# Ten low parts of a split-precision encoder layer move from VectorE to GpSimd, two units are loaded later, and three evictions are made in two steps

## The chip, the cores and the metric

The kernel runs on one core of one Trainium2 chip. The core has TensorE (PE in the profile, with its weight loads as PEld), VectorE (DVE), ScalarE (ACT), GpSimd (POOL) and SyncE (SP, which issues most DMAs here). The metric is the device time of one execution in microseconds. Before the change it is 1222.64 us, the median of three runs (1221.2 to 1223.08).

## The reference

One encoder layer over 1024 tokens of width 1024, in fp32: an adaLN-modulated norm, a gated spatial MLP and a windowed attention, merged by two gates; then the output projection `w_o`, a second norm and a SwiGLU feed-forward of width 2816. The change lies at the projection and the start of the feed-forward:

```python
mod = jax.nn.silu(c) @ w_ada + b_ada
sh1, sc1, gt1, sh2, sc2, gt2 = jnp.split(mod[:, None, :], N_MOD, axis=-1)
...
merged = jax.nn.sigmoid(gate_a) * a_out + jax.nn.sigmoid(gate_b) * b_out
x = x + gt1 * (merged @ w_o)

h2 = rmsnorm(x, norm2_g) * (1.0 + sc2) + sh2
f_gate, f_up = jnp.split(h2 @ w_ffn_in, 2, axis=-1)
x = x + gt2 * ((jax.nn.silu(f_gate) * f_up) @ w_ffn_out)
```

## The kernel before

**Split operands.** TensorE multiplies in the reduced format fp32r. Each fp32 operand is split into a high part, which ACT casts, and a low part, the operand less its high part, which DVE subtracts. `multiply` forms high times high, low times high and high times low, three matmuls of 128 by 512 for each of four slices of the contraction: one product is twelve matmuls.

**Seven products.** The large matrix multiplications are done by a seven-product scheme on 2 by 2 blocks, so sums and negated sums of blocks are formed first (also on DVE). The products are named by their token block: B11, B21, T1, T2, T3, T4 and B22. In the `w_o` stage the first two are called M1 and M2. A pair p stands for two row blocks of 128 output channels. Several products add into the same PSUM bank, and DVE reads the bank out after each of them (an eviction) into the rows of x: TensorE may start the next product on a bank only once it has been read.

**Units.** 1024 columns of weights make a unit. `fetch` loads it into one of three raw buffers, `make` adds the cast (`wh`) and the low part (`wl`), each in one of three buffers. The `w_o` stage uses the units 0, A, B and C with a number; A and C come from `sO`, sums of blocks of `w_o` that were stored earlier. It also prepares the first units of the feed-forward: g0 and g1 (the gate weights of groups 0 and 1), the raw tile of g2, and f0 and f1 (groups 4 and 5), which have a buffer of their own, called `first`, in the space of the tile T2.

**The planner.** `out_products` doesn't write down an order. It adds each operation to a `Plan` with its engine (V, A, T, D for loads on SP, G for POOL), a cost, and what it reads and writes. `Plan.order` first takes TensorE's products end to end as due times, walks back from them to a latest time for every operation, and then places operations greedily by the earliest start, ties by the latest time. The engines T and D keep the order in which they were added; V, A and G may take any ready operation. The table `COST` holds durations, `WAIT` what passes between an operation's end and its use, for loads one value, 3.4 us. The result is a fixed order per engine.

**The stage in order.** M1 and M2 for the four pairs; T2, T3 and T4 for pairs 0 and 1, then for 2 and 3; T1 and B22 in the same way. Squares of the finished rows are summed (ACT squares, DVE adds to `ss`); after the first T1 TensorE sums the columns of `ss` (`at<-ones,ss`), DVE scales the result (`ms`), POOL takes the power (`rcol`) and TensorE spreads it over the partitions (`at<-ident,rcol`, called the spread below). DVE multiplies the rows of the first half by it (`mid<-mid,mod,at`) and ACT and DVE form the high and low parts of the normed block (`h`). POOL issues the stores of the finished rows to `x1d`. Behind the plan come the first feed-forward products (f, i): (0,0), (0,1), a second pair of column sums and spread for the other half, (1,0), (1,1) to (5,1), and then (0,3), (1,3), (0,2), (1,2) and so on. `prep(f, u, part)` prepares their further units, part 0 the sums and the cast, part 1 the low part.

Most operations are recorded by one helper, so the profile puts them all at line 145, DMA issues at lines 199, 204, 1257 and 1260. The functions to look for are `Plan`, and inside `out_products` `fetch`, `make`, `accumulate` and the two loops over products, and `prep`.

Of the kernel before, what the change touches and what calls it, by code (L numbers as in the profile page):

```python
# [8 lines left out]
F32 = mybir.dt.float32  # L9
# [7 lines left out]
P = 128  # L17
# [23 lines left out]
class Plan:  # L41


    COST = {"v512": 0.6, "v1024": 1.14, "p512": 0.66, "a512": 0.52, "a1024": 0.95, "small": 0.2,
            "load": 0.4, "mm": 2.72, "few": 0.45, "pow": 1.5}
    WAIT = {"V": 0.08, "A": 0.08, "T": 0.4, "D": 3.4, "G": 0.1}

    def __init__(self):
        self.ops, self.last, self.users = [], {}, {}
# [1 line left out]
    def add(self, eng, cost, fn, reads=(), writes=()):  # L51
        n = len(self.ops)
        deps = set()
        for r in reads:
            if r in self.last:
                deps.add(self.last[r])
        for w in writes:
            deps.update(self.users.get(w, ()))
            if w in self.last:
                deps.add(self.last[w])  # L60
        for r in reads:
            self.users.setdefault(r, []).append(n)
        for w in writes:
            self.last[w], self.users[w] = n, []
        self.ops.append((eng, self.COST[cost], fn, deps))

    def order(self, free):

        n = len(self.ops)
        late = [1e9] * n  # L70
        t = 0.0
        for i, (eng, cost, _, _) in enumerate(self.ops):
            if eng == "T":
                late[i] = t
                t += cost
        for i in reversed(range(n)):
            eng, cost, _, deps = self.ops[i]
            for j in deps:
                e, c = self.ops[j][:2]
                late[j] = min(late[j], late[i] - c - self.WAIT[e])  # L80
        queues = {e: [i for i in range(n) if self.ops[i][0] == e] for e in "VATDG"}
        now = {e: free.get(e, 0.0) for e in queues}
        done, start = {}, {}
        while len(start) < n:
            best = None
            for e, q in queues.items():
                for i in q[:1] if e in "TD" else q:
                    deps = self.ops[i][3]
                    if all(j in done for j in deps):
                        at = max([now[e]] + [done[j] for j in deps])  # L90
                        key = (max(at, now[e] + 0.3), late[i], i)
                        if best is None or key < best[0]:
                            best = (key, e, i, at)
            _, e, i, at = best
            queues[e].remove(i)
            start[i] = at
            now[e] = at + self.ops[i][1]
            done[i] = now[e] + self.WAIT[e]
        return sorted(range(n), key=lambda i: (start[i], i))

    def run(self, free):
# [6 lines left out]
def kernel(  # L108
# [1380 lines left out]
    def out_products(merged):  # L1489
# [53 lines left out]
        def fetch(key, parts):  # L1543
            r = f"raw{count['raw'] % 3}"
            count["raw"] += 1

            def go():
                tiles[key] = wpool.tile([P, UNIT], F32, tag="raw", name=nm("raw"))
                for cs, src in parts:
                    load(tiles[key][:, cs], src)  # L1550
            add("D", "load", go, [], [r])
            return r

        def make(key, parts, to=None):
            r = fetch(key, parts)
            w = to
            if to is None:
                w = f"w{count['w'] % 3}"
                count["w"] += 1

            def hi():
                if key not in units:
                    units[key] = wtiles()
                A.copy(units[key][0], tiles[key])
            add("A", "a1024", hi, [r], [w + "h"])
            add("V", "v1024", lambda: split_low(tiles[key], *units[key]), [r, w + "h"], [w + "l"])
            names[key] = w

        names = {}
# [32 lines left out]
            add("T", "mm", go, [w + "h", w + "l"] + [f"{t}{x}{k}" for x in "hl" for k in KS],  # L1602
                ["b" + str(p) if b == "b" else "a" + str(p)])

        def accumulate(get, tn, p, b, sc, d):
            def go():
                t = get()
                V.scalar_tensor_tensor(out=t, in0=banks[p, b], scalar=sc[:, d : d + 1], in1=t,
                                       op0=ALU.mult, op1=ALU.add)
            add("V", "p512", go, [f"{'b' if b == 'b' else 'a'}{p}"], [tn])  # L1610

        sq = {}
        seen = set()
# [1 line left out]
        def square(get, tn, hf, d):  # L1615
            if hf not in seen:
                seen.add(hf)

                def go():
                    sq[hf] = ss_tile()[:, :HALF]  # L1620
                    A.activation(sq[hf], get(), AF.Square)
                add("A", "a512", go, [tn], ["ss"])
            else:
                q = f"t{count['t'] % 4}"
                count["t"] += 1
                key = ("q", hf, d)

                def go():
                    tiles[key] = tmp()
                    A.activation(tiles[key], get(), AF.Square)  # L1630
                add("A", "a512", go, [tn], [q])
                add("V", "v512", lambda: V.tensor_tensor(sq[hf], sq[hf], tiles[key], op=ALU.add),
                    [q], ["ss"])
            add("G", "load", lambda: store(x1d[d * P : (d + 1) * P, hf * HALF : (hf + 1) * HALF], get()),
                [tn], [f"x1d{hf}{d}"])

        need("0", 2)
# [2 lines left out]
            add("D", "load", lambda p=p: load(c11[p], x_rows(0, 2 * p)), [], [f"c{p}"])  # L1640
        blocks()
        first = [(0, "M1"), (1, "M1"), (0, "M2"), (2, "M1"), (1, "M2"), (3, "M1"), (2, "M2"), (3, "M2")]
        for n, (p, name) in enumerate(first):
            product(p, name)
            if n == 2:
                need("0", 3)
            elif n in (4, 6, 7):
                need(*{4: ("A", 0), 6: ("A", 1), 7: ("B", 0)}[n])
            accumulate(lambda p=p: c11[p], f"c{p}", p, "a" if name == "M1" else "b", gt, 2 * p)
            if name == "M2":  # L1650
                square(lambda p=p: c11[p], f"c{p}", 0, 2 * p)

# [3 lines left out]
        def new_rows(hf, q, old):  # L1656
            def go():
                if hf == 0 and q == 0:
                    h2[0] = [[hid(), hid()], [hid(), hid()]]
                (x1B if hf else h2m).append(midt(F32, 4))  # L1660
            add("D", "load", go, [], [f"{old}{k}" for k in KS] + [f"{'gh'[hf]}{d}" for d in range(4 * q, 4 * q + 4)])
            for d in range(4 * q, 4 * q + 4):
                if hf or d % 2:
                    add("D", "load", lambda d=d: load(row(hf, d), x_rows(hf, d)), [], [rn(hf, d)])

        def even_rows(q):
            for d in (4 * q, 4 * q + 2):
                add("D", "load", lambda d=d: load(row(0, d), x1d[d * P : (d + 1) * P, :HALF]),
                    [f"x1d0{d}"], [rn(0, d)])

        new_rows(1, 0, "x0")
# [9 lines left out]
        for n, (p, name) in enumerate(second):  # L1681
            product(p, name)
            if n == 2:
                need("A", 2)
            elif n == 3:
                need("A", 3)
                new_rows(1, 1, "m1")
            elif n == 5:
                need("B", 2)
                new_rows(0, 1, "x1")  # L1690
            elif n == 7:
                add("D", "load", new_firsts, [], [f"T2{x}{k}" for x in "hl" for k in KS]
                    + [f"f{i}{x}" for x in "hl" for i in range(2)])
                make(("f", 0), [(all_, w_gate[EARLY - 2])], "f0")
            elif n == 8:
                even_rows(0)
                need("C", 0)
            elif n == 9:
                make(("f", 1), [(all_, w_gate[EARLY - 1])], "f1")
                need("C", 1)  # L1700
                even_rows(1)
            elif n == 11:
                need("C", 2)
            d = 2 * p + (name != "T2")
            hf = int(name != "T4")
            accumulate(lambda hf=hf, d=d: row(hf, d), rn(hf, d), p, "a", gt if name == "T2" else ngt, d)
            if name == "T4":
                square(lambda d=d: row(0, d), rn(0, d), 0, d)

# [37 lines left out]
        for n, (p, name) in enumerate(third):  # L1747
# [15 lines left out]
            elif n == 6:  # L1763
                make(("g", 1), [(all_, w_gate[1])])
                fetch(("g", 2), [(all_, w_gate[2])])
            d = 2 * p + (name == "T1")
            accumulate(lambda d=d: row(1, d), rn(1, d), p, "c", ngt if name == "T1" else gt, d)
            square(lambda d=d: row(1, d), rn(1, d), 1, d)
        for q in range(2):
            add("T", "mm", None, [f"h{x}{k}" for x in "hl" for k in range(4 * q, 4 * q + 4)]  # L1770
                + [names["g", 0] + x for x in "hl"], [])
        add("T", "few", None, ["ss"], [])
        plan.run({"V": 2.5, "A": 1.5, "T": 0.0})
        sums.extend((sq[0], sq[1]))
        early.extend(units[k, i] for k in "fg" for i in range(2))
# [36 lines left out]
    def prep(f, u, part):  # L1812
# [11 lines left out]
            A.copy(U[f, u][0], (g, ws, ws, a22[0] if f == 0 else r[:, Q:])[u])  # L1824
            return
        h, l = U[f, u]
        V.tensor_tensor(l, (g, ws, ws, a22[0] if f == 0 else r[:, Q:])[u], h.bitcast(F32), op=ALU.subtract)
        if u == 2:
            load_gate(f + 3)
        if u == 3 and f or (f, u) == (0, 2):  # L1830
# [489 lines left out]
```

## Time and profile before

| | us |
|---|---|
| median of three runs | 1222.64 |
| the profiled execution | 1221.94 |
| its span in the profile | 1220.2 |
| PE busy | 1211.0 |
| DVE busy | 928.5 |
| ACT busy | 582.4 |
| POOL busy | 150.6 |

Rows of the timeline give the start in us from the span's start, the duration in us, engine, line, operation, tile written <- tiles read, shape and count; in brackets the idle time just before it and what ended it. Rows that are grouped by line give busy us and the mean of one in ns. Tiles in PSUM are called `mm` and `at`; all others named here lie in SBUF. A row of the table by stages gives the stretch, its length, the busy us of PE, PEld, DVE, ACT and POOL with the number of instructions, the granted clock of TensorE, the busy share of the DMA engines and GB/s.

### The profile page before, as it was taken

How to read it: one execution, taken by the hardware profiler on the slowest of the kernel's cores; microseconds unless marked ns; L12 is line 12 of the kernel's file. 1: busy time of each engine (PE TensorE's matmuls, PEld its weight loads, DVE VectorE, ACT ScalarE, POOL GpSimd, SP SyncE). 2: the span in 40 equal slices, each digit the busy share in tenths (PEclk: the TensorE clock that was granted, in tenths of full speed). 3: DMA queues.
4: the chain of work that ended last, by engine and by line, in shares of the span. 5: the costliest groups of instructions: out<-in, count | busy, mean ns of one | idle time of the engine just before them, and what ended most of it. 6: DMA issues, size and time to landing. Idle time of an engine off the chain costs nothing.

```text
span 1220.2 us, 15626 instructions
## 1 busy us (share of the span) xinstructions
PE 1211.0 (99%) x5653; PEld 1007.2 (83%) x5653; DVE 928.5 (76%) x1504; ACT 582.4 (48%) x954; POOL 150.6 (12%) x182
## 2 busy tenths in 40 slices
PE   9999999999999999999999999999999999999998
PEld 7888888888888888877888888888888888888887
DVE  8999977789978776897997767675676766765646
ACT  5667865367855443644553333333333334433341
POOL 0024323024322000001100001000000000000001
PEclk9999999999999999999999999999999999999999
DMA  9752169653277233477313446455555449995552
GB/s 363 284 180 99 35 217 358 248 216 134 104 259 240 96 117 103 148 233 266 103 49 122 172 157 223 173 192 187 190 190 199 163 155 372 394 354 190 190 172 104
DMA packets 78096, 236.54 MB, mean 194 GB/s; under 512 B 8898, under 2 KB 9154, under 8 KB 72772
## 3 DMA queue, kind: packets, MB, share of 16 engines
q1 hardware_dynamic: 63028, 163.20, 38.6%
q0 software_dynamic: 14992, 72.36, 15.8%
q8 instruction: 44, 0.72, 0.3%
q14 instruction: 32, 0.26, 0.1%
HBM read 176.28 MB, written 59.24 MB: 193 GB/s over the span
## 4 chain that ended last, share of the span: by engine, by line
PE 93%; DVE 4%; issue 1%; DMA 1%; ACT 1%; POOL 0%; SPq 0%; DVEq 0%; ACTq 0%; POOLq 0%
PE mm L145 47%; PE at L145 46%; DVE mid L145 2%; DMA raw<-in_w_q_dram 1%; DVE wl L145 1%; DMA mid<-in_xA_dram 0%; DVE ss L145 0%; DVE h L145 0%; DVE ws L145 0%; ACT wh L145 0%; DVE t L145 0%; DVE tt1l L145 0%; ACT mid L145 0%; ACT h L145 0%; DVE b22l L145 0%
## 5 line engine op out<-in xcount | busy, mean ns | idle before, releaser
L145 DVE TENSOR_TENSOR wl<-raw,wh 128x1024 fp32r<-128x1024 f32 (+1 forms) x135 | 159.0, 1182 | 61.7 <-ACT wh L145 61.1
L145 ACT CAST wh<-raw 128x1024 fp32r<-128x1024 f32 (+1 forms) x149 | 152.2, 1023 | 112.1 <-PE mm L145 39.9
L145 PE MATMUL mm<-mid,wh 128*128 128x512 f32 x640 | 197.7, 390 | 0.8 <-DVE mid L145 0.8
L145 PEld LDWEIGHTS mm<-mid,wh 128*128 128x128 f32 x640 | 119.8, 188 | 25.8 <-DVE mid L145 1.2
L145 PE MATMUL mm<-wh,h 128*128 128x512 f32 x384 | 124.7, 397 | 0.5 <-ACT h L145 0.5
L145 PE MATMUL mm<-mid,wl 128*128 128x512 f32 x320 | 124.7, 390 | 0.0
L145 PE MATMUL mm<-h,wh 128*128 128x512 f32 x304 | 94.4, 392 | 0.0
L145 PE MATMUL at<-h,wh 128*128 128x512 f32 x304 | 93.9, 390 | 0.0
L145 PEld LDWEIGHTS mm<-wh,h 128*128 128x128 f32 x384 | 70.8, 188 | 14.2 <-ACT h L145 0.9
L145 DVE TENSOR_TENSOR wl<-ws,wh 128x1024 fp32r<-128x1024 f32 (+1 forms) x54 | 60.8, 1125 | 24.2 <-ACT wh L145 24.1
L145 ACT CAST wh<-ws 128x1024 fp32r<-128x1024 f32 (+1 forms) x54 | 52.5, 973 | 42.9 <-DVE ws L145 28.0
L145 PE MATMUL mm<-wl,h 128*128 128x512 f32 x192 | 71.2, 391 | 0.0
L145 PEld LDWEIGHTS mm<-mid,wl 128*128 128x128 f32 x320 | 60.1, 188 | 12.6
L145 PEld LDWEIGHTS at<-h,wh 128*128 128x128 f32 x304 | 56.9, 188 | 11.7
L145 PEld LDWEIGHTS mm<-h,wh 128*128 128x128 f32 x304 | 56.6, 188 | 11.6
L145 ACT ACTIVATE t<-t 128x512 f32<-128x512 f32 x46 | 28.4, 631 | 71.2 <-DVE t L145 71.2
L145 DVE TENSOR_TENSOR ol<-raw,oh 128x1024 fp32r<-128x1024 f32 x30 | 36.6, 1224 | 31.4 <-ACT oh L145 29.8
L145 PE MATMUL mm<-h,wl 128*128 128x512 f32 x152 | 59.4, 391 | 0.0
L145 PE MATMUL at<-h,wl 128*128 128x512 f32 x152 | 59.3, 390 | 0.0
L145 ACT ACTIVATE xs<-xs 128x512 f32<-128x512 f32 x21 | 13.3, 632 | 94.5 <-DVE xs L145 94.5
L145 ACT CAST oh<-raw 128x1024 fp32r<-128x1024 f32 x30 | 31.6, 1053 | 44.8 <-PE at L145 21.5
L145 PE MATMUL at<-wl,wh 128*128 128x512 f32 (+1 forms) x136 | 52.7, 388 | 0.0
(296 smaller groups left out, 2882.0 us busy)
## 6 DMA issues: line engine op xcount, KB each, us to landing
mid<-in_w_ada_dram SPq DMA_DIRECT2D x28, 512.0 KB, 8.3
raw<-in_w_gate_dram SPq DMA_DIRECT2D x28, 512.0 KB, 3.7
tA<-hid POOLq DMA_DIRECT2D x11, 1024.0 KB, 4.4
tB<-hid POOLq DMA_DIRECT2D x11, 1024.0 KB, 5.0
wo<-in_w_out_dram POOLq DMA_DIRECT2D x22, 512.0 KB, 5.9
wS<-wo POOLq DMA_DIRECT2D x11, 1024.0 KB, 5.2
raw<-wS SPq DMA_DIRECT2D x44, 256.0 KB, 3.4
raw<-tB SPq DMA_DIRECT2D x44, 256.0 KB, 5.2
```

The costliest lines, as they stand in the source:

```text
L145: ins = f(*args, **kw)
```

## The change

Four edits go together.

- **Ten low parts on POOL.** In `make` the units A0, A3, C2, C3, f0 and f1 get their low part by POOL's `tensor_tensor`; in `prep` the units (0,1), (0,2), (1,1) and (1,2) do.
- **Two units later.** f0 and f1 were loaded during the second group of products (T2, T3, T4); now they are loaded during the third (T1, B22).
- **Three evictions in two steps.** The first evictions of M1 of the pairs 1, 2 and 3 read their bank by an ACT copy with the scale, and DVE then adds two SBUF tiles, instead of one DVE operation that reads PSUM.
- **Landing times by kind.** The planner's table of waits has single loads, pairs of loads, loads of rows, stores and steps without work apart; the waits are kept per operation, and due times for the first feed-forward products are added.

In the built program TensorE's instructions and their order are the same. DVE has eleven rows fewer, ACT's and DVE's orders change from the M2 products on. On SP, the loads of the four units C are no longer mixed with those of f0 and f1; the two loads of `w_up` stand ahead of C3, and g0 is followed by f0, g1, g2, f1. On POOL the ten subtractions stand between the stores of `x1d` and the two powers `rcol`: A0 ahead of all stores, A3 behind the first, C2 just ahead of the first power, C3 and f0 behind the first two stores after it, f1 two stores ahead of the second power, the other four behind it.

```diff
-            "load": 0.4, "mm": 2.72, "few": 0.45, "pow": 1.5}
-    WAIT = {"V": 0.08, "A": 0.08, "T": 0.4, "D": 3.4, "G": 0.1}
+            "load": 0.4, "pair": 0.8, "row": 0.4, "none": 0.0, "store": 0.6, "g1024": 2.35, "mm": 2.72, "few": 0.45, "pow": 1.5}
+    WAIT = {"V": 0.08, "A": 0.08, "T": 0.4, "G": 0.1, "load": 3.5, "pair": 4.8, "row": 4.6, "none": 0.0, "store": 4.0}
...
+        POOL_LOWS = (('A', 0), ('A', 3), ('C', 2), ('C', 3), ('f', 0), ('f', 1),)
...
-            add("V", "v1024", lambda: split_low(tiles[key], *units[key]), [r, w + "h"], [w + "l"])
+            if key in POOL_LOWS:
+                add("G", "g1024", lambda: G.tensor_tensor(units[key][1], tiles[key], units[key][0].bitcast(F32), op=ALU.subtract), [r, w + "h"], [w + "l"])
+            else:
+                add("V", "v1024", lambda: split_low(tiles[key], *units[key]), [r, w + "h"], [w + "l"])
...
-        def accumulate(get, tn, p, b, sc, d):
+        def accumulate(get, tn, p, b, sc, d, through=False):
+            bank = f"{'b' if b == 'b' else 'a'}{p}"
+            if through:
+                q = f"t{count['t'] % 4}"
+                count["t"] += 1
+                key = ("e", tn)
+
+                def copy():
+                    tiles[key] = tmp()
+                    A.activation(tiles[key], banks[p, b], AF.Identity, scale=sc[:, d : d + 1])
+
+                def go():
+                    t = get()
+                    V.tensor_tensor(t, tiles[key], t, op=ALU.add)
+                add("A", "a512", copy, [bank], [q])
+                add("V", "v512", go, [q], [tn])
+                return
...
+        THROUGH = (('M1', 1), ('M1', 2), ('M1', 3),)
...
-                make(("f", 0), [(all_, w_gate[EARLY - 2])], "f0")
...
-                make(("f", 1), [(all_, w_gate[EARLY - 1])], "f1")
...
+            if n == 4:
+                make(("f", 0), [(all_, w_gate[EARLY - 2])], "f0")
+            if n == 6:
+                make(("f", 1), [(all_, w_gate[EARLY - 1])], "f1")
...
+        for key in ("g", 1), None, None, None, None, ("f", 0), None, ("f", 1):
+            add("T", "mm", None, [names[key] + x for x in "hl"] if key else [], [])
...
-        V.tensor_tensor(l, (g, ws, ws, a22[0] if f == 0 else r[:, Q:])[u], h.bitcast(F32), op=ALU.subtract)
+        eng = G if (f, u) in ((0, 1), (0, 2), (1, 1), (1, 2),) else V
+        eng.tensor_tensor(l, (g, ws, ws, a22[0] if f == 0 else r[:, Q:])[u], h.bitcast(F32), op=ALU.subtract)
```

More of the change, by code (lines that the diff above doesn't have):

```diff
@@ L64, in add @@
             self.last[w], self.users[w] = n, []
-        self.ops.append((eng, self.COST[cost], fn, deps))
+        self.ops.append((eng, self.COST[cost], fn, deps, self.WAIT.get(cost, self.WAIT.get(eng))))
     def order(self, free):
@@ L71, in order @@
         t = 0.0
-        for i, (eng, cost, _, _) in enumerate(self.ops):
+        for i, (eng, cost, *_) in enumerate(self.ops):
             if eng == "T":
@@ L76, in order @@
         for i in reversed(range(n)):
[L77 to L80, printed above, removed]
+            for j in self.ops[i][3]:
+                late[j] = min(late[j], late[i] - self.ops[j][1] - self.ops[j][4])
         queues = {e: [i for i in range(n) if self.ops[i][0] == e] for e in "VATDG"}
@@ L97, in order @@
             now[e] = at + self.ops[i][1]
-            done[i] = now[e] + self.WAIT[e]
+            done[i] = now[e] + self.ops[i][4]
         return sorted(range(n), key=lambda i: (start[i], i))
@@ L1550, in go @@
                     load(tiles[key][:, cs], src)
-            add("D", "load", go, [], [r])
+            add("D", "load" if len(parts) == 1 else "pair", go, [], [r])
             return r
+        POOL_LOWS = (('A', 0), ('A', 3), ('C', 2), ('C', 3), ('f', 0), ('f', 1),)
         def make(key, parts, to=None):
@@ L1609, in go @@
                                        op0=ALU.mult, op1=ALU.add)
-            add("V", "p512", go, [f"{'b' if b == 'b' else 'a'}{p}"], [tn])
+            add("V", "p512", go, [bank], [tn])
         sq = {}
@@ L1633, in square @@
                     [q], ["ss"])
-            add("G", "load", lambda: store(x1d[d * P : (d + 1) * P, hf * HALF : (hf + 1) * HALF], get()),
+            add("G", "store", lambda: store(x1d[d * P : (d + 1) * P, hf * HALF : (hf + 1) * HALF], get()),
                 [tn], [f"x1d{hf}{d}"])
@@ L1648, in out_products @@
                 need(*{4: ("A", 0), 6: ("A", 1), 7: ("B", 0)}[n])
-            accumulate(lambda p=p: c11[p], f"c{p}", p, "a" if name == "M1" else "b", gt, 2 * p)
+            accumulate(lambda p=p: c11[p], f"c{p}", p, "a" if name == "M1" else "b", gt, 2 * p, (name, p) in THROUGH)
             if name == "M2":
@@ L1660, in go @@
                 (x1B if hf else h2m).append(midt(F32, 4))
-            add("D", "load", go, [], [f"{old}{k}" for k in KS] + [f"{'gh'[hf]}{d}" for d in range(4 * q, 4 * q + 4)])
+            add("D", "none", go, [], [f"{old}{k}" for k in KS] + [f"{'gh'[hf]}{d}" for d in range(4 * q, 4 * q + 4)])
             for d in range(4 * q, 4 * q + 4):
                 if hf or d % 2:
-                    add("D", "load", lambda d=d: load(row(hf, d), x_rows(hf, d)), [], [rn(hf, d)])
+                    add("D", "row", lambda d=d: load(row(hf, d), x_rows(hf, d)), [], [rn(hf, d)])
         def even_rows(q):
             for d in (4 * q, 4 * q + 2):
-                add("D", "load", lambda d=d: load(row(0, d), x1d[d * P : (d + 1) * P, :HALF]),
+                add("D", "row", lambda d=d: load(row(0, d), x1d[d * P : (d + 1) * P, :HALF]),
                     [f"x1d0{d}"], [rn(0, d)])
@@ L1691, in out_products @@
             elif n == 7:
-                add("D", "load", new_firsts, [], [f"T2{x}{k}" for x in "hl" for k in KS]
+                add("D", "none", new_firsts, [], [f"T2{x}{k}" for x in "hl" for k in KS]
                     + [f"f{i}{x}" for x in "hl" for i in range(2)])
-                make(("f", 0), [(all_, w_gate[EARLY - 2])], "f0")
             elif n == 8:
@@ L1705, in out_products @@
             hf = int(name != "T4")
-            accumulate(lambda hf=hf, d=d: row(hf, d), rn(hf, d), p, "a", gt if name == "T2" else ngt, d)
+            accumulate(lambda hf=hf, d=d: row(hf, d), rn(hf, d), p, "a", gt if name == "T2" else ngt, d,
+                       (name, p) in THROUGH)
             if name == "T4":
```

## The prediction

> **What bounds the kernel now.** I read the page first, then the stretch of the w_o stage by engine, then TensorE's own rows wherever it waits, and last the rows of DVE and POOL where both work at once. TensorE is busy nearly all the span:
>
> ```profile
> PE 1211.0 (99%) x5653; PEld 1007.2 (83%) x5653; DVE 928.5 (76%) x1504; ACT 582.4 (48%) x954; POOL 150.6 (12%) x182
> 500.00:525.00 25.00, 25.00 (x111) 20.32 (x110) 23.67 (x35) 19.00 (x32) 0.00 (x0) 1.00 0.50 157
> 525.00:570.00 45.00, 42.74 (x194) 34.68 (x193) 38.87 (x54) 16.17 (x21) 6.51 (x11) 1.00 0.82 280
> 570.00:590.00 20.00, 20.00 (x91) 16.31 (x89) 19.78 (x30) 13.08 (x19) 3.25 (x6) 1.00 0.38 130
> 590.00:622.00 32.00, 31.69 (x148) 26.15 (x147) 29.44 (x43) 15.05 (x23) 1.04 (x1) 1.00 0.28 94
> ```
>
> The stage rows give, in turn, PE, weight loads, DVE, ACT, POOL, clock. The clock is full, TensorE never far behind, and DVE almost full: 23.67 of 25, 19.78 of 20, 29.44 of 32. TensorE's waits in the stage:
>
> ```profile
> 530.02 0.39 PE L145 MATMUL mm<-tt2h,wl 128*128 128x512 f32 x1
> 531.18 0.74 PE L145 MATMUL mm<-mid,wh 128*128 128x512 f32 x2 [0.78 <-DVE mid L145]
> 561.05 0.39 PE L145 MATMUL mm<-tt1h,wl 128*128 128x512 f32 x1
> 561.75 1.05 PE L145 MATMUL at<-ones,ss 128*128 128x1 f32 x8 [0.31 <-DVE ss L145]
> 565.28 0.39 PE L145 MATMUL mm<-tt1h,wl 128*128 128x512 f32 x1
> 566.84 1.16 PE L145 MATMUL at<-ident,rcol 128*128 128x128 f32 x8 [1.17 <-POOL rcol L145]
> 589.40 0.39 PE L145 MATMUL at<-h,wl 128*128 128x512 f32 x1
> 589.77 1.02 PE L145 MATMUL at<-ones,ss 128*128 128x1 f32 x8
> 613.47 2.88 PE L145 MATMUL mm<-h,first 128*128 128x512 f32 x12
> 616.66 3.00 PE L145 MATMUL at<-h,first 128*128 128x512 f32 x12 [0.31 <-DVE mid L145]
> ```
>
> A product is 12 matmuls, and 613.47 plus 12 steps of 0.227 is 616.19: 2.72 us a product. Against the step of 0.227, the waits are 0.93 us before T3 of pair 0 (its bank is read by the eviction of T2), 0.47 before the first column sums, 1.33 before the spread of rcol, 0.14 before the second column sums, and 0.47 at product (5,1), which waits for the bank of the spread. With half a microsecond of cold starts behind them that is all the change can win: under 4 us.
>
> **What each edit costs.** The matmuls and their order stay the same. Ten low parts leave DVE for POOL. Three evictions lose their PSUM operand on DVE and gain a copy on ACT. The units f0 and f1 are loaded, cast and split later. The rest reorders the queues.
>
> ```profile
> L145 POOL TENSOR_TENSOR wl<-raw,wh 128x1024 fp32r<-128x1024 f32 x14 | 33.7, 2407 | 0.7
> 517.84 4.90 DVE L145 SCALAR_TENSOR_TENSOR mid<-mid,mid 128x512 f32<-128x512 f32 x8
> 522.65 1.22 DVE L145 TENSOR_TENSOR wl<-raw,wh 128x1024 fp32r<-128x1024 f32 x1
> 523.79 0.74 DVE L145 SCALAR_TENSOR_TENSOR xs<-mm,mod,xs 128x512 f32<-128x512 f32 x1
> 524.45 0.74 DVE L145 SCALAR_TENSOR_TENSOR hs<-mm,mod,hs 128x512 f32<-128x512 f32 x1
> 518.55 0.62 ACT L145 CAST mid<-mid 128x512 fp32r<-128x512 f32 x1 [2.66 <-DVE mid L145]
> 519.08 1.05 ACT L145 CAST wh<-raw 128x1024 fp32r<-128x1024 f32 x1
> L145 ACT COPY t<-mm 128x512 f32<-128x512 f32 x2 | 1.2, 583 | 0.0
> raw<-in_w_gate_dram SPq DMA_DIRECT2D x28, 512.0 KB, 3.7
> ```
>
> On DVE, from start to start, an SBUF operation of 512 columns takes 0.60 (4.90 for eight), a low part 1.14 (522.65 to 523.79), an eviction 0.66. So DVE gives up 10 x 1.14 = 11.4 us, and 3 x 0.06 by the evictions. POOL takes 2.41 each, 24 us, and has little else to do here (0.00, 6.51, 3.25 and 1.04 in the four stretches). The three copies cost ACT 0.58 each; it has 6 us free in the first 25. Two of them come ahead of A0's cast at 519.08, where ACT idles 2.66 us for DVE, and the third ahead of A1's, which DVE reaches later still: nothing. Without that idle time A0's cast would be 1.2 late. The two loads of 512 KB land 3.7 us after issue; on SP's queue they move behind the last sO units and both w_up loads, and wait for POOL to free their buffer. Their products are the last four of the first feed-forward groups, over 20 us later, so the loads themselves cost nothing. The stores of x1d now queue behind POOL's low parts by up to 2.4 us, and SP's reload of those rows waits for them, with C0 behind it; the rows are first used at the norm, C0 by T1, each some 10 us later: nothing. The landing times change only the planner's order.
>
> If that were all, I would add up the waits. It is not, because of what DVE and POOL do to each other when each reads two SBUF operands:
>
> ```profile
> 104.43 2.42 POOL L145 TENSOR_TENSOR wl<-raw,wh 128x1024 fp32r<-128x1024 f32 x1
> 104.52 1.89 DVE L145 TENSOR_TENSOR pL<-at,pH 128x512 fp32r<-128x512 f32 x3
> 106.32 0.55 DVE L145 TENSOR_TENSOR es<-rows,nmx 128x4 f32<-128x4 f32 x1
> 322.44 2.42 POOL L145 TENSOR_TENSOR wl<-raw,wh 128x1024 fp32r<-128x1024 f32 x1
> 323.73 1.15 DVE L145 TENSOR_TENSOR es<-rows,nmx 128x4 f32<-128x4 f32 x1
> 122.92 0.16 DVE L145 TENSOR_TENSOR es<-rows,nmx 128x4 f32<-128x4 f32 x1
> 304.84 1.28 POOL L145 TENSOR_TENSOR mid<-xs,mid 64x512 fp32r<-64x512 f32 x1 [4.71 <-ACT mid L145]
> 330.04 1.28 DVE L145 TENSOR_TENSOR t<-t,rows 128x512 f32<-128x512 f32 x2
> 330.86 1.61 POOL L145 TENSOR_TENSOR mid<-xs,mid 64x512 fp32r<-64x512 f32 x1 [3.79 <-ACT mid L145]
> ```
>
> The tiny es sum takes 0.16 alone. Started inside a POOL low part it takes 0.55 and 1.15, and ends when POOL does: 106.87 against 106.85, 324.88 against 324.86. The three pL operations, whose first operand lies in PSUM, run beside the same POOL operation at their usual 0.60. The other way round, POOL's 1.28 becomes 1.61 behind a pair of DVE operations on SBUF. So a POOL low part stops DVE's SBUF operations until it ends, and waits for them to begin. The 14 low parts that POOL already has lie beside PSUM reads; the ten new ones lie in a stage where most DVE work (low parts, sums, negated sums) reads SBUF twice. Each then costs DVE between nothing (all beside evictions and scalings) and 2.41, and saves 1.14.
>
> What stays open is when POOL gets in while DVE runs such operations back to back. At 330.86 it came in the second of a pair and waited to the end of the run. I take that: POOL enters at DVE's next PSUM operation, which it then overlaps, so 1.75 us of block (2.41 less 0.66). The other end, entry at the next operation's end, is a rival.
>
> The sum, along TensorE. A0 is cast by 520.1; DVE streams to 522.65, so POOL runs from 522.7 to 525.1. Behind it DVE has four lows of T3 and three of T4 (0.60 each), the lows of A1 and B0 (1.14) and T2's eviction: 7 x 0.60 + 2 x 1.14 + 0.66 = 7.14, to 532.25; T3 starts at 532.4 instead of 531.18: +1.2. A3 enters beside the eviction of T3 of pair 1 and ends at 542.0; five SBUF operations, six evictions and the low of B2 (3.0 + 3.96 + 1.14) then reach 550.1, while TensorE is ready for T3 of pair 2 at 548.8: +1.4. C2 starts when T4 of pair 3 is evicted and stored, 562.6, some 0.2 before the last sum of squares is ready; the sum waits until 565.0, and the column sums start 1.95 late instead of 0.47: +1.5. The spread of rcol no longer waits, since nothing slow stands before it on DVE: -1.3. Then DVE has 23 operations of 0.66, seven of 0.60 and two low parts to the last sum of squares of the other half, 21.7 us from 569.7, with 1.8 of block by C3, 1.75 by f1, none by f0 (it falls on scalings) and 0.4 of small waits: 595.4. TensorE, from the spread at 569.5, with eight products and 0.3 before B22 of pair 2, is there at 592.5: +0.3 and +2.9, less 0.1 that it waits there today. In the feed-forward groups two of the four lows fall before the last use of the spread; with 1.14 saved and some 1.2 blocked each, (5,1) waits as today: 0. Together 1.2 + 1.4 + 1.5 - 1.3 + 0.3 + 2.8 = +5.9.
>
> The profiled execution took 1221.94 us for its span of 1220.2; the median of the three runs is 1222.64, 0.7 above, and I set the sum on the median: 1228.5 us.
>
> The Trainium skill (SBUF — State Buffer, Who interferes with whom) says that a DVE instruction with two SBUF inputs contends with a GpSimd instruction that reads SBUF, and that whichever issues first keeps the pair for its whole length. The es rows agree; on a run of DVE operations no row here decides, and by that rule POOL would enter at the next operation's end, which is the second rival.
>
> **Rivals.** First, faster: DVE loses no more than it saves, because the blocks fall on evictions, scalings and idle time. Then DVE reaches T2's eviction at 529.8 and T3 starts at 530.66 (0.5 won); the sums are in time (0.5), rcol too (1.3), (5,1) as well with its cold start (0.6), and 0.1: 3.0, so 1219.6 us. It decides where the block per low part is under 1.14 us. For it speaks f0, against it the es rows. Chance 0.18.
>
> Second, POOL enters at every operation's end. A0 then blocks 2.4 instead of 1.8 (T3 +1.9), and C3 and f0 run back to back inside the four lows of h, so T1's eviction ends at 585.4 and B22 of pair 2 waits 3.4 instead of 0.3: 5.9 + 0.7 + 3.1 + 0.5 in the chain, 1232.8 us. Chance 0.25.
>
> Third, little changes: races go the other way. If C2 starts behind the last sum (a matter of 0.2 us) and f1's split falls in a break of DVE, 1.5 and 2.4 go: +2.0, 1224.6 us. Chance 0.12.
>
> **The numbers.** My forecast has 0.45, its own range is 1225.5 to 1232. What counts as the same is 0.2%, 2.4 us. The forecast and the second rival are slower (0.70), the third the same (0.12), the first faster (0.18). The range goes from 1219.0, to take in the first rival, to 1233.5, for the second.
>
> **What would show it.** POOL should have ten operations of 2.4 us, or longer where DVE holds them up, between 520 and 635. DVE operations on two SBUF tiles that start inside them should last to their end, evictions not. T3 of pair 0 should start near 532.4 by DVE, the first column sums wait 2 us for ss, the spread wait for nothing, the second column sums near 595 wait 3 us for ss. The prediction fails if DVE's operations inside POOL's keep 0.60, or if the planner's new order places them all beside PSUM reads.

## The result and the profile after

The changed kernel takes 1229.28 us (median of six runs, 1228.14 to 1231.04), the kernel before 1223.08 us beside it: a ratio of 1.0052, 95% interval 1.0037 to 1.0066. The forecast was 1228.5 us, slower with a chance of 0.70. The profiled execution took 1228.14 us for a span of 1226.4; before, the span was 1220.2.

The busy line of the page and the table by stages of the changed kernel (same columns as before):

```profile
PE 1212.5 (99%) x5653; PEld 1007.8 (82%) x5653; DVE 933.7 (76%) x1494; ACT 584.2 (48%) x957; POOL 180.4 (15%) x192
500.00:525.00 25.00, 25.00 (x111) 20.25 (x109) 23.89 (x34) 20.03 (x34) 4.73 (x1) 1.00 0.55 172
525.00:570.00 45.00, 43.11 (x194) 34.93 (x195) 36.63 (x51) 15.02 (x21) 12.15 (x13) 1.00 0.73 249
570.00:590.00 20.00, 17.44 (x71) 13.97 (x70) 19.97 (x22) 11.97 (x16) 11.30 (x7) 0.91 0.39 132
590.00:622.00 32.00, 30.23 (x141) 24.64 (x139) 29.77 (x39) 14.31 (x22) 7.28 (x6) 1.00 0.38 123
```

DVE gave up ten low parts of 1.14 us (1494 instructions are left of 1504), and is busier than before (933.7 against 928.5). In 570 to 590 it has 22 instructions instead of 30 and is as full as before. TensorE lost 2.6 us there, and its granted clock fell to 0.91.

TensorE's own rows at the places that the prediction named:

```profile
528.41 0.50 PE L143 MATMUL mm<-tt2h,wl 128*128 128x512 f32 x1 [0.44 <-DVE wl L143]
...
530.59 0.39 PE L143 MATMUL mm<-tt2h,wl 128*128 128x512 f32 x1
532.02 0.73 PE L143 MATMUL mm<-mid,wh 128*128 128x512 f32 x2 [1.05 <-DVE mid L143]
...
549.04 0.73 PE L143 MATMUL mm<-mid,wh 128*128 128x512 f32 x2 [0.40 <-DVE mid L143]
...
562.55 0.39 PE L143 MATMUL mm<-tt1h,wl 128*128 128x512 f32 x1
562.78 0.95 PE L143 MATMUL at<-ones,ss 128*128 128x1 f32 x8
...
578.03 0.39 PE L143 MATMUL mm<-tt1h,wl 128*128 128x512 f32 x1
580.98 0.80 PE L143 MATMUL mm<-b22h,wh 128*128 128x512 f32 x1 [2.56 <-DVE mid L143]
581.57 0.63 PE L143 MATMUL mm<-b22l,wh 128*128 128x512 f32 x1
...
584.13 0.40 PE L143 MATMUL mm<-b22l,wh 128*128 128x512 f32 x1
...
593.24 0.39 PE L143 MATMUL at<-h,wl 128*128 128x512 f32 x1
595.28 0.91 PE L143 MATMUL at<-ones,ss 128*128 128x1 f32 x7 [1.66 <-DVE ss L143]
...
619.00 2.88 PE L143 MATMUL mm<-h,first 128*128 128x512 f32 x12
623.07 1.17 PE L143 MATMUL at<-h,first 128*128 128x512 f32 x4 [1.19 <-DVE mid L143]
```

Against the step of 0.227: 0.60 for a low part inside T2 of pair 1 (528.41), 1.20 before T3 of pair 0, 0.56 before T3 of pair 2 (549.04), nothing at the first column sums, 2.72 before B22 of pair 2, 1.81 at the second column sums, 1.35 at (5,1); the spread of rcol doesn't wait either. Behind the 2.72 seven matmuls go at half rate: from 580.98 to 584.13 are 3.15 us for seven steps, 1.56 more than at full clock. The second column sums start 5.51 late (595.28 against 589.77), (5,1) 6.41 late (623.07 against 616.66), and the span ends 6.2 late.

The same places on POOL and DVE:

```profile
517.70 4.90 DVE L143 SCALAR_TENSOR_TENSOR mid<-mid,mid 128x512 f32<-128x512 f32 x8
520.14 4.73 POOL L143 TENSOR_TENSOR wl<-raw,wh 128x1024 fp32r<-128x1024 f32 x1 [128.79 <-ACT wh L143]
522.52 0.74 DVE L143 SCALAR_TENSOR_TENSOR xs<-mm,mod,xs 128x512 f32<-128x512 f32 x1
523.18 4.04 DVE L143 TENSOR_TENSOR mid<-mid,mid 128x512 fp32r<-128x512 f32 x4
...
561.70 0.69 DVE L143 TENSOR_TENSOR ss<-ss,t 128x512 f32<-128x512 f32 x1 [0.70 <-ACT t L143]
561.86 2.78 POOL L143 TENSOR_TENSOR wl<-raw,wh 128x1024 fp32r<-128x1024 f32 x1
...
570.18 7.03 DVE L143 SCALAR_TENSOR_TENSOR h<-mid,mod,h 128x512 fp32r<-128x512 f32 x4
571.44 2.41 POOL L143 TENSOR_TENSOR wl<-raw,wh 128x1024 fp32r<-128x1024 f32 x1 [3.20 <-ACT wh L143]
573.81 2.85 POOL L143 TENSOR_TENSOR first<-raw,first 128x1024 fp32r<-128x1024 f32 x1
...
585.40 2.06 DVE L143 SCALAR_TENSOR_TENSOR h<-mid,mod,h 128x512 fp32r<-128x512 f32 x3
586.11 4.22 POOL L143 TENSOR_TENSOR first<-raw,first 128x1024 fp32r<-128x1024 f32 x1 [1.05 <-ACT first L143]
587.39 3.49 DVE L143 TENSOR_TENSOR ss<-ss,t 128x512 f32<-128x512 f32 x2
```

A0's low part (520.14) takes 4.73: it waits until DVE's run of negated sums ends and the eviction at 522.52 reads PSUM, and then holds up the four low parts behind it, 4.04 instead of some 2.5. C2's (561.86) begins just after the last sum of squares has begun, which keeps 0.69. C3's and f0's lie back to back inside the four low parts of h: 7.03 instead of 2.73. f1's, ready at 586.11, gets in between two sums of squares: 3.49 instead of 1.41. A blocked operation shows as a long one, with no idle time before it. C2's blocks nothing; each of the other nine on POOL, those of the feed-forward groups included, stretches one DVE operation by 1.5 to 2.2. Together that is 16.5 us against the 11.4 that DVE gave up, and so DVE is 5.2 us busier.

### The profile page after: what moved, and what is told of

Its sections match the earlier page's. It is cut to its first block, busy times and chain, and to the rows that moved or that the text cites. A ratio compares the mean times of both kernels' runs of the same rounds, so it can differ in the third digit from the quotient of the medians.

```text
span 1226.4 us, 15636 instructions
## 1 busy us (share of the span) xinstructions
PE 1212.5 (99%) x5653; PEld 1007.8 (82%) x5653; DVE 933.7 (76%) x1494; ACT 584.2 (48%) x957; POOL 180.4 (15%) x192
## 4 chain that ended last, share of the span: by engine, by line
PE 88%; DVE 7%; DMA 3%; issue 1%; ACT 0%; SPq 0%; DVEq 0%; ACTq 0%
PE at L143 45%; PE mm L143 43%; DVE mid L143 3%; DMA mid<-in_w_ada_dram 1%; DVE ss L143 1%; DVE h L143 1%; DMA raw<-in_w_q_dram 1%; DMA raw<-in_w_ada_dram 1%; DVE b22l L143 1%; DVE wl L143 0%; DMA mid<-in_xA_dram 0%; DVE t L143 0%; DVE hs L143 0%; DVE tt1l L143 0%; DVE raw L143 0%
## 5 line engine op out<-in xcount | busy, mean ns | idle before, releaser
L143 DVE TENSOR_TENSOR wl<-raw,wh 128x1024 fp32r<-128x1024 f32 (+1 forms) x131 | 154.2, 1180 | 59.0 <-ACT wh L143 54.6
L143 DVE TENSOR_TENSOR wl<-ws,wh 128x1024 fp32r<-128x1024 f32 (+1 forms) x50 | 55.9, 1117 | 24.8 <-ACT wh L143 24.8
L143 POOL TENSOR_TENSOR wl<-raw,wh 128x1024 fp32r<-128x1024 f32 x18 | 46.6, 2586 | 133.6 <-ACT wh L143 132.9
```

The lines of the kernel that those rows point to most:

```text
L143: ins = f(*args, **kw)
```

## The experiments

Each ratio below is to the kernel before, timed beside it, with its 95% interval.

**All ten low parts on DVE**, the rest of the change kept.

```diff
-        POOL_LOWS = (('A', 0), ('A', 3), ('C', 2), ('C', 3), ('f', 0), ('f', 1),)
+        POOL_LOWS = ()
...
-        eng = G if (f, u) in ((0, 1), (0, 2), (1, 1), (1, 2),) else V
+        eng = V
```

> All ten low parts go back to DVE; the later loads of f0 and f1, the three evictions in two steps and the planner's new tables stay. If the POOL low parts stop DVE (my theory), the whole loss goes: 1221.5 to 1224 us, and DVE's operations on SBUF keep their usual durations (0.60 for 512 columns, 1.14 for 1024). If the later loads, the new order of the queues or the two-step evictions cost the time (rival), it stays at 1227 us or above.

Measured 1222.96 us, ratio 1.0003 (0.9994 to 1.0012). The loss is gone and DVE is busy 927.9 us. That the rest is neutral as a whole doesn't say that each part of it is; the later runs take it apart. The plan of the stage is made anew in each of these kernels, so a difference holds the new order too; the blocks themselves are read from the long operations above and from the benches below.

**Six on POOL, or four.** First the second line of that diff alone, then the first alone.

> The four low parts of the feed-forward groups go back to DVE, the six of the w_o stage stay on POOL. My theory: TensorE's path up to the second column sums is as in the changed kernel (5.5 us late), only the wait at (5,1), 1.35 instead of 0.47, goes back: 1228 to 1229 us. If every POOL low costs the same, 4 tenths of 6.2 go: 1226.8 us.

> The six low parts of the w_o stage go back to DVE, the four of the feed-forward groups stay on POOL. My theory: DVE is not behind when these four come, so the loss is at most the 0.9 us seen at (5,1): 1222 to 1224.5 us. If every POOL low costs the same, 4 tenths of 6.2: 1225.6 us.

Six: 1226.74 us, ratio 1.0037 (1.0024 to 1.0049). Four: 1223.75 us, 1.0010 (0.9999 to 1.0021). The first missed the forecast of 1228 to 1229. The w_o stage is as in the changed kernel (second column sums at 595.39), but behind it two waits go, not one: the 1.35 at (5,1), and 0.61 at product (1,3), where TensorE waits for `hs` by DVE and which I had not looked at. The 1226.74 is what the rival said (every low part costs the same), and the interval overlaps that of the changed kernel; for the four the same rival's 1225.6 failed. In the trace the four lengthen the wait at (5,1) from 0.89, with all ten on DVE, to 1.45; their time can't be told from the kernel before. So the six make most of the loss.

**Without C3 and f0 on POOL**, the pair that lies inside the low parts of h.

```diff
-        POOL_LOWS = (('A', 0), ('A', 3), ('C', 2), ('C', 3), ('f', 0), ('f', 1),)
+        POOL_LOWS = (('A', 0), ('A', 3), ('C', 2), ('f', 1),)
```

> C3's and f0's low parts go back to DVE, the other eight stay on POOL. My theory: the four low parts of h take 2.7 us on DVE again instead of 7.0; DVE gives 2.3 for the two low parts instead of 4.3 of block, so B22 of pair 2 waits under 0.8 instead of 2.7, TensorE stays at full clock behind it, and the last sum of squares comes 2 us earlier: 1226.5 to 1227.5 us. If the slow matmuls behind B22 of pair 2 have another cause than the wait ahead of them, they stay at 0.43 us a step.

Measured 1225.68 us, ratio 1.0022 (1.0012 to 1.0031). DVE's low parts of h and TensorE's stretch in this kernel:

```profile
570.24 1.41 DVE L143 SCALAR_TENSOR_TENSOR h<-mid,mod,h 128x512 fp32r<-128x512 f32 x2
572.71 1.41 DVE L143 SCALAR_TENSOR_TENSOR h<-mid,mod,h 128x512 fp32r<-128x512 f32 x2
570.00:590.00 20.00, 19.36 (x86) 15.70 (x84) 19.92 (x29) 12.95 (x18) 3.24 (x6) 1.00 0.37 132
```

Four times 0.7 again, no wait before B22 of pair 2, no half-rate matmuls, clock 1.00. So here the slow matmuls went with the wait ahead of them. It gained 0.8 us more than forecast; the planner also moved f1's low part to 594.40, behind the second power on POOL, where DVE stands idle, so this run took three blocks out of the stretch and not two.

**Each low part in two halves.**

```diff
-                add("G", "g1024", lambda: G.tensor_tensor(units[key][1], tiles[key], units[key][0].bitcast(F32), op=ALU.subtract), [r, w + "h"], [w + "l"])
+                def halves():
+                    for cs in (slice(0, UNIT // 2), slice(UNIT // 2, UNIT)):
+                        G.tensor_tensor(units[key][1][:, cs], tiles[key][:, cs], units[key][0][:, cs].bitcast(F32), op=ALU.subtract)
+                add("G", "g1024", halves, [r, w + "h"], [w + "l"])
```

(and the same in `prep`)

> The changed kernel with each of the ten POOL low parts made in two operations of 512 columns instead of one of 1024. If POOL gets in at DVE's next PSUM operation or break and overlaps it (my theory), a half of 1.2 us behind an eviction of 0.66 blocks 0.55, two halves 1.1 instead of 1.75, and DVE can pass between them: 1226 to 1228 us. If a POOL low blocks DVE for its whole length wherever it stands, the halves block as long together: 1229 us.

Measured 1227.75 us (1225.28 to 1229.75), ratio 1.0034 (1.0021 to 1.0047): inside the range of my theory, but its interval overlaps that of the changed kernel, so the times don't decide. In the trace A0's halves still hold up the four low parts behind them to 4.05. C3's and f0's stretch those of h to 4.82 instead of 7.03, and the sum of squares and the low part behind them to 1.12 and 2.30; B22 of pair 2 waits 2.04 instead of 2.72, and runs at full clock. A halved operation does let DVE through, but the second column sums start at 595.25, where they started before.

**Bench: who blocks whom.** Behind the last matmuls of the kernel before, a DVE sum releases one POOL operation, and DVE goes on with a run of one kind. The output is not touched, and the time of the whole means nothing.

```diff
+        sb = lambda: V.tensor_tensor(z0, z1, z0, op=ALU.add)
+        lo = lambda: G.tensor_tensor(yy[:, :UNIT], xx[:, :UNIT], xx[:, UNIT:], op=ALU.subtract)
+        cp = lambda: G.tensor_copy(yy[:, :UNIT], xx[:, :UNIT])
+        ms = lambda: G.memset(yy[:, :UNIT], 0.0)
...
+        for dve, pool_op in (([sb] * 8, None), ([sb] * 8, lo), ([sb] * 16, lo), ([sb] * 8, cp), ([sb] * 8, ms),
...
+            V.tensor_tensor(xx[:, :512], yy[:, :512], xx[:, :512], op=ALU.add)
+            if pool_op:
+                pool_op()
+            for f in dve:
+                f()
```

> The kernel before, with a bench of 60 to 80 us put behind its last matmuls: a DVE sum of 512 columns releases one POOL operation of 1024 columns, and DVE goes on with 8 operations of 512 columns of one kind (16 in one case). My theory: eight sums of two SBUF tiles keep 4.9 us and the POOL subtraction waits for all of them (start to end 7 us behind eight, 12 us behind sixteen); eight operations with a PSUM operand keep 5.3 and POOL its 2.41; with four sums and then four PSUM operations POOL enters at the fifth. Alternating sums and PSUM operations lose 1.75 us in all. Rival: POOL enters behind the first sum and the rest lose 2.4. A POOL copy that reads one tile (1.04) and a POOL memset that reads none should block nothing if it is the second SBUF operand that counts; DVE operations with one SBUF operand and ACT copies should run beside the POOL subtraction.

Its rows, DVE's run of eight sums first alone, then with POOL's subtraction, copy and memset:

```profile
1225.82 5.76 DVE L145 TENSOR_TENSOR zz<-zz 128x512 f32<-128x512 f32 x8
1232.10 7.79 DVE L145 TENSOR_TENSOR zz<-zz 128x512 f32<-128x512 f32 x8
1232.27 2.71 POOL L145 TENSOR_TENSOR yy<-xx 128x1024 f32<-128x1024 f32 x1 [23.85 <-DVE xx L145]
1254.52 6.48 DVE L145 TENSOR_TENSOR zz<-zz 128x512 f32<-128x512 f32 x8
1254.67 1.43 POOL L145 COPY yy<-xx 128x1024 f32<-128x1024 f32 x1 [11.39 <-DVE xx L145]
1261.52 5.77 DVE L145 TENSOR_TENSOR zz<-zz 128x512 f32<-128x512 f32 x8
```

The subtraction costs DVE 2.03 us, the copy of one tile 0.72, the memset nothing. So my expectation failed: POOL came in behind the first sum (its 2.71 is 2.41 and the rest of that sum), with four sums and then four PSUM operations too, and it is enough that POOL reads one SBUF tile. Each case was run once. The Trainium skill (SBUF — State Buffer, Who interferes with whom) says that DVE with two SBUF inputs contends with a GpSimd instruction that reads SBUF; copy and memset agree. In this bench each sum needed the one before it, and they started 0.72 us apart instead of the kernel's 0.60.

**Second bench**, with DVE's operations of a run going to four slices in turn.

```diff
-        sb = lambda: V.tensor_tensor(z0, z1, z0, op=ALU.add)
+        z = lambda k: zz[:, 512 * (k % 4) : 512 * (k % 4) + 512]
+        w = lambda k: aa[:, 512 * (k % 4) : 512 * (k % 4) + 512]
+        sb = lambda k: V.tensor_tensor(z(k), z(k), w(k), op=ALU.add)
```

> The first bench again, but DVE's operations of a run go to four slices in turn, as in the kernel, so none needs the one just before it (in the first bench each did, and started 0.71 us apart instead of 0.60; there POOL got in behind the first sum and cost the run 2.0 us). Theory A: POOL gets in only where DVE pauses or reads PSUM, so here it waits out the whole run of sums (POOL 5 to 7 us behind eight, over 10 behind sixteen) and DVE loses nothing. Theory B: it gets in at the next operation's end, and the run loses 2.4 us as before. Runs with a PSUM operand, with one SBUF operand and ACT copies should be as long with the POOL subtraction as without. Two halves among alternating sums and PSUM operations should cost nothing, the whole operation 1.2 us.

DVE's runs with POOL's subtraction beside them, once with its copy: eight sums, sixteen sums, eight sums with the copy, eight operations with a scale from a column and two SBUF tiles, eight with a PSUM operand, eight with one SBUF operand, four sums ahead of four PSUM operations, then one sum between PSUM operations beside a whole subtraction, and one beside a halved one:

```profile
1231.85 4.89 DVE L145 TENSOR_TENSOR zz<-zz,aa 128x512 f32<-128x512 f32 x8
1232.01 6.93 POOL L145 TENSOR_TENSOR yy<-xx 128x1024 f32<-128x1024 f32 x1 [22.98 <-DVE xx L145]
1239.58 11.85 DVE L145 TENSOR_TENSOR zz<-zz,aa 128x512 f32<-128x512 f32 x16
1251.96 4.89 DVE L145 TENSOR_TENSOR zz<-zz,aa 128x512 f32<-128x512 f32 x8
1252.11 5.65 POOL L145 COPY yy<-xx 128x1024 f32<-128x1024 f32 x1 [9.64 <-DVE xx L145]
1264.30 7.46 DVE L145 SCALAR_TENSOR_TENSOR zz<-aa,mod,zz 128x512 f32<-128x512 f32 x8
1278.16 5.34 DVE L145 SCALAR_TENSOR_TENSOR zz<-at,mod,zz 128x512 f32<-128x512 f32 x8
1287.31 2.75 DVE L145 TENSOR_SCALAR zz<-aa 128x512 f32<-128x512 f32 x8
1287.53 4.74 POOL L145 TENSOR_TENSOR yy<-xx 128x1024 f32<-128x1024 f32 x1 [6.81 <-DVE xx L145]
1292.91 4.63 DVE L145 TENSOR_TENSOR zz<-zz,aa 128x512 f32<-128x512 f32 x4
...
1307.61 2.16 DVE L145 TENSOR_TENSOR zz<-zz,aa 128x512 f32<-128x512 f32 x1
...
1314.74 0.86 DVE L145 TENSOR_TENSOR zz<-zz,aa 128x512 f32<-128x512 f32 x1
```

Beside eight sums POOL waits for the whole run (6.93) and DVE loses nothing: theory A. Beside sixteen it came in behind the first, and the run takes 11.85 where 16 x 0.60 and a last 0.08 make 9.7: 2.15 lost, theory B. The four sums ahead of PSUM operations, which theory A would have let pass, take 4.63 where 2.5 is usual: POOL came in behind the first again. The copy waits out its eight sums (5.65), and DVE loses nothing. Eight operations with a scale column take 5.38 alone and 7.46 here. A run with a PSUM operand takes 5.34 with and without POOL, ACT's eight copies 4.25 with and without. The run with one SBUF operand keeps its 2.75 too, but POOL waits for its end (4.74). Between PSUM operations a sum loses 1.49 to a whole subtraction and, twice, 0.19 to a halved one, where I had set 1.2 and nothing. So both theories hold in some runs: what POOL does once it is in is settled, and what decides whether it gets into a run of sums is not.

**The later loads.** From the kernel with all low parts on DVE, f0 and f1 go back to the second group of products; then the same edit on the changed kernel, with its ten low parts on POOL.

```diff
             elif n == 7:
...
+                make(("f", 0), [(all_, w_gate[EARLY - 2])], "f0")
...
             elif n == 9:
+                make(("f", 1), [(all_, w_gate[EARLY - 1])], "f1")
...
-            if n == 4:
-                make(("f", 0), [(all_, w_gate[EARLY - 2])], "f0")
-            if n == 6:
-                make(("f", 1), [(all_, w_gate[EARLY - 1])], "f1")
```

> All ten low parts on DVE, and f0 and f1 loaded, cast and split in the second group of products again as in the kernel before; the three evictions in two steps and the planner's new tables stay. My theory: the later loads cost nothing, so it equals the kernel with all low parts on DVE, 1223 us. Rival: with f0 and f1 late, their casts and low parts come at the second column sums, where TensorE waits 1.2 us for ss and 1.4 us for t; with them early these waits go: 1220 to 1221.5 us.

> The changed kernel with f0 and f1 loaded, cast and split in the second group of products again; the ten low parts stay on POOL. If the later loads cost 2.8 us beside POOL's low parts too, as they did with all low parts on DVE, 1226.5 us; if POOL's blocks decide alone, f0 and f1 block in the second group instead of the third and the time stays at 1228 to 1230 us.

The first takes 1220.18 us, ratio 0.9975 (0.9967 to 0.9984): faster than both kernels of this study. The second takes 1225.51 us, 1.0026 (1.0016 to 1.0036). In both cases the later loads cost 0.26 to 0.28%, some 3 us. How, with the low parts on DVE, two rows of the kernel with late loads show:

```profile
591.93 1.05 ACT L143 CAST first<-raw 128x1024 fp32r<-128x1024 f32 x1 [4.26 <-DMA raw<-in_w_gate_dram]
600.49 0.73 PE L143 MATMUL at<-h,wh 128*128 128x512 f32 x2 [1.27 <-DVE t L143]
```

ACT waits 4.26 us for f1's load, and behind that cast, in ACT's fixed order, stand a silu and the next cast; DVE makes `t` late, and TensorE waits 1.27 for its bank. With early loads TensorE has no wait there, and none at (5,1), where it waits 0.89 with late ones. In the changed kernel the mechanism is another: f0's low part comes in among those of h, behind C3's. With early loads only C3's does (the four take 4.88), B22 of pair 2 waits 0.57, and the clock stays at 1.00.

**Two-step evictions.** The kernel with low parts on DVE and early loads, its evictions in one step again; then the kernel before with the three evictions in two steps alone.

```diff
-        THROUGH = (('M1', 1), ('M1', 2), ('M1', 3),)
+        THROUGH = ()
```

> As the run before, and the three evictions of M1 in one DVE operation again: of the whole change only the planner's tables are left. My theory: the two-step evictions cost and give nothing, so it equals the run with f0 and f1 early within 0.5 us. If they relieve DVE ahead of T3 of pair 0, this run is 0.5 to 1 us slower than that one.

> The kernel before with nothing but the three evictions in two steps. If the evictions themselves were worth the 5.4 us between the last two runs of the batch before, it would be near 1217.5 us. If that was the planner's order with the new tables (my theory: there C0's cast waited behind f1's, which waited for its load), it stays within 1 us of the kernel before, 1222 to 1224 us.

Without them, with only the planner's tables left of the change: 1225.6 us, ratio 1.0024 (1.0012 to 1.0036). Alone on the kernel before: 1220.21 us, 0.9983 (0.9974 to 0.9991). So they gain 2.1 us by themselves, outside the 1 us that I had allowed, and 0.49% (6 us) where the new tables alone had lost 0.24%. The kernel with the tables alone varies most, from 1223.04 to 1228.64, so the 6 us is less sure than its sign: the two profiled executions, both at full clock, differ by 4.6. ACT's cast of C2 in the kernel before, in the kernel with the two-step evictions alone, and ACT's cast of f1 in the one with the tables alone:

```profile
563.29 1.05 ACT L145 CAST wh<-raw 128x1024 fp32r<-128x1024 f32 x1 [2.92 <-DMA raw<-sO]
```

```profile
561.43 1.04 ACT L145 CAST wh<-raw 128x1024 fp32r<-128x1024 f32 x1 [1.05 <-DMA raw<-sO]
```

```profile
558.12 1.05 ACT L143 CAST first<-raw 128x1024 fp32r<-128x1024 f32 x1 [6.51 <-DMA raw<-in_w_gate_dram]
```

With the two-step evictions alone C2's loads land earlier and its cast comes 1.86 us earlier; its low part, which stands ahead of the scaling of the column sums on DVE in both kernels, follows it, and the spread of rcol starts at 565.20 without its 1.33 of wait; the first column sums lose their 0.47 too. With the tables alone ACT stands idle 6.51 us for f1's load while C0's cast waits behind it, and the first column sums start at 566.12. The wait that an eviction itself could shorten is as before: TensorE waits 0.88 before T3 of pair 0 with the two-step evictions, 0.93 without. So the gain lies, as far as these rows show, in the order of loads and casts that the planner makes of the changed costs; which of the moved loads brings it was not tried.

## Why the prediction was right

The time was right (1228.5 against 1229.28), and so was its main reason: POOL's low parts stop DVE, and all ten back on DVE give 1222.96. The forecast sum for the ten was 5.9 us. With late loads they cost 1.0052 against 1.0003, with early loads 1.0026 against 0.9975: 0.49 and 0.51%, some 6 us. But two steps beside it were wrong, and that they cancelled, so that the sum for the ten fits the whole change, is luck.

- "The loads themselves cost nothing": they cost some 3 us. The step looked at when the products need f0 and f1, and not at what stands behind f1's cast on ACT or where f0's low part falls.
- Copies of the two-step evictions: "nothing". With the planner's tables they gain 3.1 us together (the kernel with low parts on DVE and early loads, 0.9975), by another order of loads and casts. "The landing times change only the planner's order" was true and priced wrongly: by the runs such an order is worth 2 to 3 us either way.

Term by term, along TensorE:

- **T3 of pair 0.** POOL entered A0's low part at the eviction, as I had it, and T3 started at 532.02 (forecast 532.4, by DVE). A part of the delay came before: the wait of 0.60 inside T2 of pair 1, which the sum hadn't.
- **T3 of pair 2**: wrong in size: it waits 0.56 by DVE `mid`, where the forecast added 1.4 to the 1.2 of pair 0; the start is 1.36 late in all (549.04 against 547.68).
- **First column sums, +1.5**: wrong. The last sum of squares began at 561.70 and C2's low part at 561.86, so the sums didn't wait. This race of 0.2 us was in the third rival.
- **Spread, -1.3**: right.
- **B22 of pair 2, +0.3**: wrong, it waited 2.72, and its start at half rate cost 1.56 more. "None by f0 (it falls on scalings)" failed: C3 and f0 ran back to back inside the low parts of h, which the second rival had said, with a wait of 3.4.
- **Second column sums, +2.8**: the time was right, 595.28 against 595.4. But that is luck: DVE began this stretch at 567.54 and not 569.7, since the first column sums had cost nothing, and its blocks were 4.3 in the low parts of h and 2.1 by f1 where I had 1.8 and 1.75. Along TensorE the forecast 0.3 by B22 of pair 2 became 4.3, and the smaller terms around it (this one is 1.67) make up for that.
- **(5,1), 0**: wrong, 1.35 instead of 0.47, and 0.61 at (1,3). Each of these low parts on POOL stretched one DVE operation by some 1.7 to 1.9 us, where I had set 1.2.

The assumption that carried the sum, entry at DVE's next PSUM operation, held for A0 and failed for C3 and f0; the rival that took the next operation's end held for these and failed for A0. f1's fits neither: it let the low parts of h end, and came in behind the first of two sums of squares. The first rival (under 1.14 of block per low part) is excluded by the ten low parts' 6 us.

## What to carry to other kernels

Before work goes from DVE to POOL, list what DVE does beside it: here operations with two SBUF operands stopped for as long as POOL read SBUF, operations that read PSUM didn't, and POOL's idle share said nothing of it. A low part that saves DVE 1.14 us and blocks it for 1.5 to 2.2 is a loss wherever DVE sets the pace. When several edits go together and a planner orders the work, measure each alone: here the evictions with the tables gained some 3 us, the later loads lost some 3 and the low parts 6, and the sum looked like the last.

## What the hardware showed that I had not expected

- After a wait of 2.72 us TensorE ran at half rate, for seven steps in 3.15 us. The row of the clock (eighth number):

```profile
582.00:584.00 2.00, 2.00 (x6) 1.62 (x5) 2.00 (x4) 1.72 (x4) 0.15 (x1) 0.50 0.55 221
```

  After 2.04 us (the halved low parts, B22 of pair 2) it did not, after 3.35 us (the same run, second column sums) it did, with steps of 0.43 from 596.8 to 599.8. The Trainium skill (TensorE: Matmul & The Clock Gate, Part 1) gives half rate after an idle window of about 3.4 us; the half rate agrees, and here 2.72 was enough. But the length of a wait doesn't decide it: in the second bench's trace, which up to there is the kernel before, a wait of 1.38 us ahead of the first column sums, eight matmuls of one column, was followed by half rate from 564.97 to 568.38, and in the changed kernel with early loads it came at 27.16 behind sixteen such matmuls with no wait at all. Each of these stretches lasted 3.41 us; what starts one these runs don't show.
- A POOL copy that reads one tile stopped DVE's sums as well once it was in (0.72 us in the first bench; in the second it waited the run out), a POOL memset didn't.
- DVE operations with one SBUF operand, 0.34 us each when they are independent, kept POOL out until their end.
